# One encoder layer in fp32 on one core: the third group's gMLP split around the prompt output projections, an input of the FFN modulated early, low parts on VectorE

## The chip, the core and the metric

The kernel runs on one core of one Trainium2 chip. The metric is the device time of one execution in microseconds; the median of the runs is given. "TensorE", "VectorE", "ScalarE", "GpSimd" and "SP" are the engines that the profile calls PE, DVE, ACT, POOL and SP.

## What is computed

One layer of a bidirectional encoder, for a prompt of 1024 tokens and a sample of 512 with separate conditions `c` and the same weights. Model width 1024, 12 attention heads of 64 in three dilation groups, four gMLP groups of 64 channels, FFN width 2816. Cut to what matters:

```
h    = rms_norm(x, g_pre_mix) * (1 + sc1) + sh1
proj = h @ w_in                              # q, k, v of the heads; gu, gv of the gMLP
attn = dilated window attention, heads weighted by a softmax over the groups' denominators
gm   = gelu(gu) * (W_s @ layer_norm(gelu(gv)) + b_s)      # in chunks of 128 positions
mix  = concat(attn, gm) @ w_out
x    = x + gt1 * rms_norm(mix, g_post_mix)   # "x1" below
h    = rms_norm(x, g_pre_ffn) * (1 + sc2) + sh2
f    = (silu(h @ w_gate) * (h @ w_up)) @ w_down
y    = x + gt2 * rms_norm(f, g_post_ffn)
```

## The kernel before

**Groups and products.** The 1536 tokens are three groups of 512: 0 and 1 are the prompt, 2 is the sample. Activations lie as eight chunks of 128 channels by 512 tokens. Each fp32 product is made of three matmuls of operands in two parts: `split` (L139) casts the source to the high part on ScalarE (L140) and subtracts it from the source for the low part, on VectorE unless GpSimd is named (L141). Weights are loaded into `wraw`, split into `whl` and used in three matmuls a piece (L158). A matmul's weights, moving operand and result are named in the trace as `pmm<-h,whl`.

**Around the change.** After the attention of group 2 come, on TensorE: the output projection of group 0 (`out_proj(0)`), that of group 1, the whole gMLP of group 2, `out_proj(2)`, and then the first half of the FFN (`ffn_up`). The FFN's first product goes over both prompt groups by a Winograd scheme of seven products of half size: `wino_in` makes its inputs.

- `gmlp` (L728): the v projection (96 matmuls of 128x256), gelu, a normalisation and a split on VectorE, ScalarE and GpSimd (L752 to L762); then the u projection (48 matmuls of 128x512), the mixing over positions (32 matmuls `pst<-qk`), sums (L784), the gate (L787, L791) and two stores into `mix` in DRAM (L792).
- `mix_in` (L867): for each of eight chunks it loads `mix`, for six of them also a reciprocal `rden` and multiplies (L872), then splits into the operands of an output projection, the low part on GpSimd.
- `out_proj` and `post` (L795): eight tiles of the product, evacuated scaled (L808) and squared (L809), the squares summed (L192). A generator goes on in the background: it takes the root, multiplies the eight tiles by it (L821), loads the input, adds it (L822), stores `x1` (L823), squares and sums (L839). At its end stands the root for the FFN's normalisation, `rs2`.
- `wino_in` (L897): for both prompt groups it spreads `rs2`, loads the chunks of `x1`, multiplies them by the root on VectorE (L910), scales and shifts them on ScalarE (L911), forms four sums and differences (`sub`, L894) and splits five of the seven operands (`keep`), three of them with the low part on GpSimd. The other two are stored in DRAM and loaded and split later (`wino_late`).

**What sets the order.** The program is written for a scheduler that puts instructions on each engine in the order of their emission and priority. Background work is a list of generators, `self.back`; `tick(n)` advances the first of them n steps and goes to the next when it is exhausted, and tick(-1) drains all. Tiles come from rings with a fixed number of buffers: three of `xc` (all chunk loads), two of `tb`, two pairs of `st`, four each of `whl` and `wraw`. A load into a ring waits until the tile three (or two, or four) before is done with. SP issues all loads and stores in one order. Later `ada_rest` steps (the conditions' projection, `self.ada`) are filled in between.

## Time and profile before

| | us |
|---|---|
| median of three runs (1874.41, 1874.43, 1877.22) | 1874.43 |
| the profiled execution | 1874.75 |
| its span | 1873.0 |
| TensorE busy | 1808.1 |
| VectorE busy | 1046.9 |
| ScalarE busy | 692.8 |
| GpSimd busy | 145.5 |

The profiled execution is 1.75 us longer than its span. Its mean granted TensorE clock is 0.978. Times of the rows below count from the start of the span. The places: the sample attention ends near 592 us, `out_proj(0)` near 622, `out_proj(1)` at 670, the v and u projections of the third group run from 670 to 694, the mixing from 707 to 719, `out_proj(2)` from 719 to 777, and the FFN after that.

### The profile page before, as it was taken

The page shows a single profiled execution, that of the slowest core. Times are in us where ns is not written, and L with a number is a line of the kernel's source. Part 1 is how long each engine was busy: PE and PEld are TensorE (multiplying, and loading weights), DVE is VectorE, ACT ScalarE, POOL GpSimd, SP SyncE. Part 2 cuts the span into 40 slices and gives each one's busy share as a digit, 9 for nine tenths or more (in the row PEclk, how much of TensorE's full clock was granted, in tenths as well). Part 3 has the DMA queues.
Part 4 walks back from the last instruction along what each step waited for, and adds up shares of the span by engine and source line. Part 5 has one row for each costly group of instructions (what it writes and reads, how often), then busy time and mean ns, then how long its engine had stood idle before and what let it go on. Part 6 is the DMA issues. An engine that isn't in the chain of part 4 may idle for free.

```text
span 1873.0 us, 23145 instructions
## 1 busy us (share of the span) xinstructions
PE 1808.1 (97%) x8602; PEld 1431.1 (76%) x8602; DVE 1046.9 (56%) x1655; ACT 692.8 (37%) x1192; POOL 145.5 (8%) x98
## 2 busy tenths in 40 slices
PE   7999999999999987899999999999999999999997
PEld 7777876776777876677778888878887888888886
DVE  4333964573675566995566766663375374444223
ACT  3611642152335454742232322343345333333232
POOL 0400200010131003400000000000002000000001
PEclk9999999999999997899999999999999999999998
DMA  8112223233363445563321222264365342222432
GB/s 342 34 57 79 91 84 107 102 115 124 102 212 130 136 167 191 181 206 128 111 94 70 79 90 74 73 203 143 103 207 182 96 169 94 92 96 92 139 93 76
DMA packets 125985, 232.47 MB, mean 124 GB/s; under 512 B 14000, under 2 KB 19376, under 8 KB 125872
## 3 DMA queue, kind: packets, MB, share of 16 engines
q1 hardware_dynamic: 125728, 230.93, 36.9%
q8 instruction: 67, 1.10, 0.2%
q14 instruction: 46, 0.38, 0.1%
q10 hardware_dynamic: 144, 0.07, 0.0%
HBM read 196.86 MB, written 34.08 MB: 123 GB/s over the span
## 4 chain that ended last, share of the span: by engine, by line
PE 82%; DVE 7%; DMA 4%; issue 4%; ACT 1%; POOL 1%; DVEq 0%; SPq 0%; POOLq 0%; ACTq 0%
PE pmm L158 66%; PE ppv L158 9%; PE pst L158 7%; DMA xc<-hid 2%; DVE whl L141 1%; DVE sc L587 1%; POOL h L141 1%; DMA xc<-rden 1%; DMA xc<-in_x 1%; DVE sd L587 0%; DVE sc L821 0%; DMA xc<-x 0%; DVE h L141 0%; DVE st L910 0%; DVE acc L192 0%
## 5 line engine op out<-in xcount | busy, mean ns | idle before, releaser
L158 PE MATMUL pmm<-h,whl 128*128 128x512 f32 (+1 forms) x3813 | 946.1, 401 | 13.9 <-ACT h L140 4.6
L158 PEld LDWEIGHTS pmm<-h,whl 128*128 128x128 f32 x3813 | 712.7, 190 | 205.6 <-issue 21.2
L141 DVE TENSOR_TENSOR whl<-wraw,whl 128x512 fp32r<-128x512 f32 (+1 forms) x424 | 293.4, 696 | 315.1 <-ACT whl L140 314.8
L140 ACT CAST whl<-wraw 128x512 fp32r<-128x512 f32 (+1 forms) x424 | 255.9, 607 | 504.9 <-PE pmm L158 373.7
L158 PE MATMUL pmm<-qk,whl 128*128 128x512 f32 x798 | 202.1, 396 | 1.7 <-DVE whl L141 1.6
L158 PEld LDWEIGHTS pmm<-qk,whl 128*128 128x128 f32 x798 | 150.1, 189 | 38.2 <-DVE whl L141 3.0
L158 PE MATMUL ppv<-h,whl 128*128 128x512 f32 x396 | 100.0, 395 | 0.0
L158 PE MATMUL pmm<-v,whl 128*128 128x512 f32 x342 | 90.3, 396 | 0.7 <-DVE st L986 0.7
L158 PEld LDWEIGHTS ppv<-h,whl 128*128 128x128 f32 x396 | 74.5, 188 | 17.5
L158 PE MATMUL pst<-qk 64*128 64x128 f32 (+3 forms) x384 | 65.8, 336 | 17.3 <-DVE qk L141 17.3
L158 PE MATMUL pmm<-h,sc 128*128 128x512 f32 x315 | 80.5, 394 | 0.0
L158 PEld LDWEIGHTS pmm<-v,whl 128*128 128x128 f32 x342 | 64.3, 189 | 18.6 <-ACT whl L140 2.5
L158 PEld LDWEIGHTS pst<-qk 64*128 64x128 f32 (+1 forms) x384 | 48.8, 201 | 38.0 <-issue 32.9
L158 PEld LDWEIGHTS pmm<-h,sc 128*128 128x128 f32 x315 | 59.2, 188 | 13.8
L158 PE MATMUL pmm<-vm,whl 128*128 128x512 f32 x225 | 64.5, 402 | 4.2 <-ACT whl L140 3.9
L192 DVE TENSOR_TENSOR acc<-acc,ta 128x512 f32<-128x512 f32 x55 | 37.8, 687 | 52.3 <-ACT ta L809 42.6
L140 ACT CAST whl<-sd 128x512 fp32r<-128x512 f32 x53 | 32.7, 619 | 83.2 <-PE ppv L158 53.7
L218 POOL TENSOR_TENSOR rq<-rq,half 128x4 f32<-128x4 f32 (+1 forms) x11 | 11.8, 1072 | 585.7 <-DVE rq L217 585.7
L158 PEld LDWEIGHTS pmm<-vm,whl 128*128 128x128 f32 x225 | 42.2, 191 | 18.9 <-ACT whl L140 5.9
L197 POOL PARTITION_ALL_REDUCE acc<-acc x2 | 7.1, 3544 | 578.5 <-DMA xc<-hid 519.3
L462 DVE SCALAR_TENSOR_TENSOR sc<-cst,pst 128x512 f32<-128x512 f32 (+2 forms) x56 | 26.9, 512 | 38.5 <-PE pst L158 38.4
L141 DVE TENSOR_TENSOR whl<-sd,whl 128x512 fp32r<-128x512 f32 x53 | 36.5, 689 | 20.6 <-ACT whl L140 20.6
(241 smaller groups left out, 2012.2 us busy)
## 6 DMA issues: line engine op xcount, KB each, us to landing
wraw<-in_wgu SPq DMA_DIRECT2D x132, 256.0 KB, 2.6
wraw<-in_wdn SPq DMA_DIRECT2D x120, 256.0 KB, 2.6
wraw<-in_win SPq DMA_DIRECT2D x84, 256.0 KB, 2.8
xc<-in_wada SPq DMA_DIRECT2D x48, 256.0 KB, 3.4
wraw<-in_wout SPq DMA_DIRECT2D x48, 256.0 KB, 2.8
sd<-in_wgu SPq DMA_DIRECT2D x44, 256.0 KB, 3.5
xc<-hid SPq DMA_DIRECT2D x44, 256.0 KB, 3.0
xc<-in_x SPq DMA_DIRECT2D x40, 256.0 KB, 3.4
```

The lines of the kernel that those rows point to most:

```text
L140: self.nc.scalar.copy(hi, src)
L141: (eng or self.nc.vector).tensor_tensor(out=lo, in0=src, in1=hi.bitcast(F32), op=ALU.subtract)
L158: self.nc.tensor.matmul(out, lhsT, rhs, start=start, stop=stop, skip_group_check=True)
L192: nc.vector.tensor_tensor(out=acc, in0=acc, in1=t, op=ALU.add)
L197: self.nc.gpsimd.partition_all_reduce(ss, ss, channels=128, reduce_op=RED.add)
L218: nc.gpsimd.tensor_tensor(out=y, in0=y, in1=self.half8[:, :n], op=ALU.pow)
L462: self.nc.vector.scalar_tensor_tensor(out=out, in0=table, scalar=slope, in1=ps, op0=ALU.mult, op1=ALU.add)
L587: nc.vector.tensor_tensor(out=o, in0=o, in1=m, op=ALU.subtract)
```

## The change

1. `gmlp` becomes `gmlp_norm` (v projection, gelu, normalisation, split) and `gmlp_mix` (u projection, mixing, store). For group 2 the first is called right after the sample attention, ahead of `out_proj(0)`, the second after `out_proj(1)`. Groups 0 and 1 call both at once, as before.
2. A new generator, `wino_early`, loads the eight chunks of group 0's `x1`, multiplies them by its root on VectorE, scales and shifts them on ScalarE, into `tb`, and stores them in DRAM (`early`). `wino_in` loads group 0's half from there and modulates group 1's alone (`modulated`).
3. The rest of the `ada` steps and two ticks stand ahead of `out_proj(1)`, and `wino_early` and `mix_in(2)` are put into the background list ahead of it. Before, `mix_in(2)` was put there behind it.
4. The low parts of `mix_in(1)` and `mix_in(2)`, and of three of the five operands in `wino_in`, are made on VectorE: 8 + 8 + 12 instructions. Those of `mix_in(0)` stay on GpSimd.
5. `mix_in(1)` takes its tiles from other rings: three of `qk`, three of `v`, two of `vm`, instead of six and two.

```diff
--- before.py
+++ after.py
@@ -92,6 +92,7 @@
         self.rden = self.dr.tile([NG, 2, 128, TG], F32, name="rden")
         self.x1 = self.dr.tile([NG, 128, KC, TG], F32, name="x1")
         self.hid = self.dr.tile([2, NJ, 128, TG], F32, name="hid")
+        self.early = self.dr.tile([KC, 128, TG], F32, name="early")
         self.late = self.dr.tile([2, 4, 128, TG], F32, name="late")
         self.h = {}
         self.rs2 = {}
@@ -726,6 +727,9 @@
         return t
 
     def gmlp(self, gi, steps):
+        self.gmlp_mix(gi, self.gmlp_norm(gi, steps), steps)
+
+    def gmlp_norm(self, gi, steps):
         nc = self.nc
         self.gmlp_constants()
         wv = [self.weights(self.a["wgv"][i], share=SHARE[2]) for i in range(2)]
@@ -763,6 +767,10 @@
             vh = self.t("qk", [128, 8, 2, 64], F32R)
             self.split(vh[:, :, 0], vh[:, :, 1], w3)
             vhs.append(vh)
+        return vhs
+
+    def gmlp_mix(self, gi, vhs, steps):
+        nc = self.nc
         us = []
         for j in range(2):
             w = self.weights(self.a["win"][18 + j], share=SHARE[2])
@@ -864,14 +872,14 @@
                 eng.tensor_tensor(out=y, in0=y, in1=xs[j][:, :, o], op=ALU.add)
                 nc.sync.dma_start(out=dst[:, 2 * j:2 * j + 2, o], in_=y)
 
-    def mix_in(self, gi, hs, kcs=range(KC), tags=("h",) * KC):
+    def mix_in(self, gi, hs, kcs=range(KC), tags=("h",) * KC, eng=None):
         for kc in kcs:
             x = self.load_chunk(self.mix[gi, kc])
             if kc < 6:
                 r = self.load_chunk(self.rden[gi, kc % 2])
                 self.nc.vector.tensor_tensor(out=x, in0=x, in1=r, op=ALU.mult)
             h = self.t(tags[kc], [128, 2, 512], F32R)
-            self.split(h[:, 0], h[:, 1], x, self.nc.gpsimd)
+            self.split(h[:, 0], h[:, 1], x, eng)
             hs.append(h)
             yield
 
@@ -893,42 +901,53 @@
     def sub(self, out, a, b, eng=None):
         (eng or self.nc.vector).tensor_tensor(out=out, in0=a, in1=b, op=ALU.subtract)
 
+    def wino_early(self):
+
+        rs = self.spread(self.rs2[0], True)
+        for kc in range(KC):
+            x = self.load_chunk(self.x1[0, :, kc])
+            t = self.t2("tb")
+            self.modulated(t, x, rs, kc)
+            self.nc.sync.dma_start(out=self.early[kc], in_=t)
+            yield
+
+    def modulated(self, t, x, rs, kc):
+        self.nc.vector.tensor_tensor(out=t, in0=x, in1=rs, op=ALU.mult)
+        self.nc.scalar.activation(t, t, AF.Identity, bias=self.mod[:, 3, kc, 0:1], scale=self.G[2][:, kc, 0:1])
+
     def wino_in(self, ops):
 
         nc = self.nc
-        rs = [self.spread(self.rs2[gi], True) for gi in range(2)]
+        rs = self.spread(self.rs2[1], True)
         for o in ("B11", "T2", "B21", "T3", "T1", "T4", "B22"):
             ops[o] = []
         for k in range(4):
             B = {}
             for kk in range(2):
                 pair = self.t("st", [128, 2, 512])
-                for gi in range(2):
-                    kc = k + 4 * kk
-                    x = self.load_chunk(self.x1[gi, :, kc])
-                    t = pair[:, gi]
-                    nc.vector.tensor_tensor(out=t, in0=x, in1=rs[gi], op=ALU.mult)
-                    nc.scalar.activation(t, t, AF.Identity, bias=self.mod[:, 3, kc, 0:1], scale=self.G[2][:, kc, 0:1])
-                    B[kk, gi] = t
+                kc = k + 4 * kk
+                nc.sync.dma_start(out=pair[:, 0], in_=self.early[kc])
+                self.modulated(pair[:, 1], self.load_chunk(self.x1[1, :, kc]), rs, kc)
+                B[kk, 0], B[kk, 1] = pair[:, 0], pair[:, 1]
                 yield
             B11, B12, B21, B22 = B[0, 0], B[0, 1], B[1, 0], B[1, 1]
             T = self.t("sd", [128, 3, 512])
             T1, T2 = T[:, 0], T[:, 1]
 
-            def keep(o, src, eng):
+            def keep(o, src):
                 h = self.t(self.OPS[5 * k + ("B11", "T2", "B21", "T3", "T1").index(o)], [128, 2, 512], F32R)
-                self.split(h[:, 0], h[:, 1], src, eng)
+                self.split(h[:, 0], h[:, 1], src)
                 ops[o].append(h)
-            keep("B11", B11, nc.gpsimd)
+            keep("B11", B11)
             self.sub(T1, B12, B11)
             self.sub(T2, B22, T1)
-            keep("T2", T2, nc.vector)
+            keep("T2", T2)
             yield
-            keep("B21", B21, nc.gpsimd)
+            keep("B21", B21)
             self.sub(B12, B22, B12)
-            keep("T3", B12, nc.vector)
+            keep("T3", B12)
             yield
-            keep("T1", T1, nc.gpsimd)
+            keep("T1", T1)
             self.sub(B21, B21, T2)
             nc.sync.dma_start(out=self.late[0, k], in_=B21)
             nc.sync.dma_start(out=self.late[1, k], in_=B22)
@@ -1122,16 +1141,18 @@
         hs = [[], [], []]
         for sp in range(2):
             if sp:
-                self.back.append(self.mix_in(0, hs[0]))
+                self.back.append(self.mix_in(0, hs[0], eng=self.nc.gpsimd))
             self.attention_slot(self.S, sp, STEPS[1])
         self.tick(-1)
-        self.back.append(self.mix_in(1, hs[1], tags=["qk"] * 6 + ["v"] * 2))
+        vhs = self.gmlp_norm(2, GS)
+        self.back.append(self.mix_in(1, hs[1], tags=["qk"] * 3 + ["v"] * 3 + ["vm"] * 2))
         self.out_proj(0, hs[0], 4)
-        self.out_proj(1, hs[1], 4)
         for _ in self.ada:
             pass
-        self.back.append(self.mix_in(2, hs[2], range(6)))
-        self.gmlp(2, GS)
+        self.tick(2)
+        self.back += [self.wino_early(), self.mix_in(2, hs[2], range(6))]
+        self.out_proj(1, hs[1], 4)
+        self.gmlp_mix(2, vhs, GS)
         self.tick(-1)
         for _ in self.mix_in(2, hs[2], range(6, 8)):
             pass
```

The new file's lines are one higher up to L726, then 4, then 8 and more: L821, L822 and L839 become L829, L830 and L847, L872 becomes L880, L894 becomes L902, L910 becomes L915.

How the order of the instructions moves, at three places. First TensorE at the end of the sample attention; `ppv<-sc,v` are its PV products, `pst<-cst,vm` transpositions, `pmm<-h,whl` products of `out_proj(0)`, `pmm<-whl,h` products of the v projection. Before:

```order
L158 MATMUL pmm<-h,whl 128x512 x11
L158 MATMUL ppv<-sc,v 64x192
L158 MATMUL ppv<-sc,ones_82 64x192
L158 MATMUL pmm<-h,whl 128x512 x6
L551 MATMUL pst<-cst,vm 128x128 x4
L158 MATMUL pmm<-h,whl 128x512 x4
L158 MATMUL ppv<-sc,v 64x192
```

Changed:

```order
L159 MATMUL pmm<-whl,h 128x256 x10
L159 MATMUL ppv<-sc,v 64x192
L159 MATMUL ppv<-sc,ones_83 64x192
L159 MATMUL pmm<-whl,h 128x256 x9
L552 MATMUL pst<-cst,vm 128x128 x4
L159 MATMUL pmm<-whl,h 128x256 x11
L159 MATMUL ppv<-sc,v 64x192
```

The v projection of the third group stands between the PV products where products of the first output projection stood.

Second, VectorE behind the u projection of the third group. `xc<-xc` are the multiplications of mix chunks by `rden`, `acc` the gate of the gMLP, `tb<-xc,rs` the modulations of `wino_early`, `h<-xc,h` low parts of mix chunks, and `sc<-sc,rs` the multiplications of the second prompt group. Before:

```order
L787 SCALAR_TENSOR_TENSOR st<-st,row 128x512 x2
L791 SCALAR_TENSOR_TENSOR acc<-st,acc 128x512
L872 TENSOR_TENSOR xc<-xc 128x512
L217 TENSOR_SCALAR rq<-pst 128x4
L723 TENSOR_TENSOR acc<-acc,pmm 128x512
L872 TENSOR_TENSOR xc<-xc 128x512
L725 SCALAR_TENSOR_TENSOR acc<-acc,pmm 128x512
L791 SCALAR_TENSOR_TENSOR acc<-st,acc 128x512
L872 TENSOR_TENSOR xc<-xc 128x512
L141 TENSOR_TENSOR whl<-wraw,whl 128x512 x3
L910 TENSOR_TENSOR st<-xc,rs 128x512 x2
```

Changed:

```order
L915 TENSOR_TENSOR tb<-xc,rs 128x512
L724 TENSOR_TENSOR acc<-acc,pmm 128x512
L915 TENSOR_TENSOR tb<-xc,rs 128x512
L726 SCALAR_TENSOR_TENSOR acc<-acc,pmm 128x512
L880 TENSOR_TENSOR xc<-xc 128x512
L799 SCALAR_TENSOR_TENSOR acc<-st,acc 128x512
L142 TENSOR_TENSOR h<-xc,h 128x512
L880 TENSOR_TENSOR xc<-xc 128x512
L142 TENSOR_TENSOR h<-xc,h 128x512
L142 TENSOR_TENSOR v<-st,v 128x512
L880 TENSOR_TENSOR xc<-xc 128x512
L829 TENSOR_TENSOR sc<-sc,rs 128x512 x8
```

The last of the eight early modulations stand ahead of the first mix chunk, and the eight multiplications of `post(1)` behind the third; before, those and the residual adds stood ahead of the chunks.

Third, SP, which issues the loads into `xc`: `xc<-in_x` are the inputs of the residual adds of `post(1)`, `x_68<-sc` its stores of `x1`, `xc<-x_68` loads of `x1` for `wino_in`. Before:

```order
L239 DMA xc<-in_x 128x512
L823 DMA x_68<-sc 128x512
L239 DMA xc<-mix 128x512
L823 DMA x_68<-sc 128x512
L239 DMA xc<-rden 128x512
L239 DMA xc<-mix 128x512
L239 DMA xc<-rden 128x512
L239 DMA xc<-mix 128x512
L239 DMA xc<-rden 128x512
L239 DMA xc<-mix 128x512
L239 DMA xc<-rden 128x512
L239 DMA xc<-mix 128x512
```

Changed:

```order
L831 DMA x_68<-sc 128x512 x2
L240 DMA xc<-in_x 128x512
L831 DMA x_68<-sc 128x512
L240 DMA xc<-in_x 128x512 x2
L151 DMA wraw<-in_wout 128x512
L831 DMA x_68<-sc 128x512 x2
L240 DMA xc<-mix 128x512
L831 DMA x_68<-sc 128x512
L240 DMA xc<-mix 128x512
L240 DMA xc<-x_68 128x512 x3
```

Before, the loads of the residual adds are followed by those of the mix chunks; now the last two of the eight mix chunks are loaded behind the residual adds, and the loads of `wino_in` behind them.

## Rows read from the trace of the kernel before

**Rows 1.** The page's first part: busy time of each engine, its share of the span, and its number of instructions.

```profile
PE 1808.1 (97%) x8602; PEld 1431.1 (76%) x8602; DVE 1046.9 (56%) x1655; ACT 692.8 (37%) x1192; POOL 145.5 (8%) x98
```

**Rows 2.** The windows of 20 us around the change: window, its length, busy time of PE, PEld, DVE, ACT and POOL with the number of instructions, the granted clock of TensorE (1.00 is 2.4 GHz, 0.50 is 1.2 GHz), the busy share of the DMA engines, GB/s.

```profile
700.00:720.00 20.00, 8.17 (x35) 7.84 (x36) 15.04 (x30) 8.47 (x15) 5.71 (x4) 0.50 0.68 213
...
740.00:760.00 20.00, 15.90 (x62) 12.17 (x61) 16.99 (x24) 15.59 (x27) 9.47 (x4) 0.91 0.58 197
...
780.00:800.00 20.00, 14.62 (x55) 11.27 (x55) 19.50 (x27) 14.68 (x28) 7.41 (x5) 0.74 0.51 170
800.00:820.00 20.00, 16.21 (x58) 12.60 (x59) 19.30 (x33) 8.02 (x14) 0.00 (x0) 0.83 0.54 185
820.00:840.00 20.00, 19.65 (x86) 15.59 (x85) 20.00 (x35) 8.64 (x15) 0.00 (x0) 1.00 0.69 237
```

**Rows 3.** The timeline of TensorE over the same stretch: start, length, engine, line, operation, what it writes from what, shape, count; in brackets the wait ahead of it and what ended it.

```profile
707.17 3.65 PE L158 MATMUL pst<-qk 128*128 128x128 f32 x16 [12.67 <-DVE qk L141]
715.48 3.65 PE L158 MATMUL pst<-qk 128*128 128x128 f32 x16 [4.66 <-DVE qk L141]
...
749.58 0.73 PE L158 MATMUL pmm<-h,whl 128*128 128x512 f32 x2 [3.31 <-ACT whl L140]
751.10 26.46 PE L158 MATMUL pmm<-h,whl 128*128 128x512 f32 x106 [0.79 <-DVE whl L141]
...
784.55 1.84 PE L158 MATMUL pst<-ones,acc 128*128 128x2 f32 x8 [4.93 <-DVE acc L192]
...
803.05 1.22 PE L158 MATMUL pmm<-vm,whl 128*128 128x512 f32 x2 [3.29 <-ACT whl L140]
...
829.86 0.50 PE L158 MATMUL pmm<-vm,whl 128*128 128x512 f32 x1 [0.35 <-DVE whl L141]
```

**Rows 4.** The timeline of VectorE, columns as before: the multiplications (L821) and residual adds (L822) of the second prompt group, the mix chunks' products (L872), the first modulation of the Winograd inputs (L910), eight multiplications of the third group, and the low part that ends TensorE's wait at 829.86. Then a row of GpSimd's timeline: the low part of the last mix chunk.

```profile
693.33 1.88 DVE L822 TENSOR_TENSOR sc<-sc,xc 128x512 f32<-128x512 f32 x3
...
709.71 0.69 DVE L822 TENSOR_TENSOR sc<-sc,xc 128x512 f32<-128x512 f32 x1 [0.80 <-DMA xc<-in_x]
...
714.04 0.69 DVE L872 TENSOR_TENSOR xc<-xc 128x512 f32<-128x512 f32 x1 [0.20 <-DMA xc<-rden]
...
732.58 0.69 DVE L872 TENSOR_TENSOR xc<-xc 128x512 f32<-128x512 f32 x1 [1.96 <-DMA xc<-rden]
...
740.56 1.94 DVE L910 TENSOR_TENSOR st<-xc,rs 128x512 f32<-128x512 f32 x2 [2.66 <-DMA xc<-x]
...
799.47 4.89 DVE L821 TENSOR_TENSOR sc<-sc,rs 128x512 f32<-128x512 f32 x8
...
829.12 0.68 DVE L141 TENSOR_TENSOR whl<-wraw,whl 128x512 fp32r<-128x512 f32 x1
...
740.06 1.29 POOL L141 TENSOR_TENSOR h<-xc,h 128x512 fp32r<-128x512 f32 x1 [3.19 <-ACT h L140]
```

**Rows 5.** Groups of like instructions between 670 and 845 us: line, engine, operation, output from input, shapes, count, then busy time and mean ns of one, and the idle time before them. At the end the row of GpSimd's timeline and of VectorE's that meet.

```profile
L911 ACT ACTIVATE st<-st,mod,G 128x512 f32<-128x512 f32 x16 | 12.6, 813 | 8.9 <-DVE st L910 8.9
L910 DVE TENSOR_TENSOR st<-xc,rs 128x512 f32<-128x512 f32 x16 | 12.5, 807 | 3.8 <-DMA xc<-x 3.1 <-DMA late<-st 0.7
...
L894 DVE TENSOR_TENSOR st<-st,sd 128x512 f32<-128x512 f32 x4 | 4.9, 1226 | 0.0
L894 DVE TENSOR_TENSOR st<-st 128x512 f32<-128x512 f32 x4 | 4.9, 1224 | 0.0
...
L894 DVE TENSOR_TENSOR sd<-st 128x512 f32<-128x512 f32 x4 | 3.8, 950 | 1.0 <-ACT st L911 1.0
...
L894 DVE TENSOR_TENSOR sd<-sd 128x512 f32<-128x512 f32 x4 | 2.7, 680 | 0.0
...
L894 DVE TENSOR_TENSOR ta<-wraw 128x512 f32<-128x512 f32 x2 | 2.4, 1214 | 0.0
...
761.21 1.74 POOL L141 TENSOR_TENSOR qk<-st,qk 128x512 fp32r<-128x512 f32 x1
...
761.71 1.78 DVE L894 TENSOR_TENSOR st<-st 128x512 f32<-128x512 f32 x1
```

**Rows 6.** TensorE's timeline at the end of the second prompt group's output projection: the first part of the third group's v projection, and its u projection.

```profile
669.95 4.73 PE L158 MATMUL pmm<-whl,h 128*128 128x256 f32 x38
...
683.09 11.41 PE L158 MATMUL pmm<-h,whl 128*128 128x512 f32 x48
```

**Rows 7.** The tail of the sample attention: TensorE's timeline (PV products `ppv` among products of the first output projection `pmm`), then two low parts of VectorE's.

```profile
567.96 2.80 PE L158 MATMUL pmm<-h,whl 128*128 128x512 f32 x11
...
572.16 1.67 PE L158 MATMUL pmm<-h,whl 128*128 128x512 f32 x6
...
572.25 0.68 DVE L141 TENSOR_TENSOR whl<-wraw,whl 128x512 fp32r<-128x512 f32 x1
...
576.09 0.68 DVE L141 TENSOR_TENSOR whl<-wraw,whl 128x512 fp32r<-128x512 f32 x1
```

**Rows 8.** DMA issues between 560 and 830 us: output from input, queue, kind, count, KB each, median us from issue to landing.

```profile
xc<-mix SPq DMA_DIRECT2D x11, 256.0 KB, 2.5
late<-st SPq DMA_DIRECT2D x8, 256.0 KB, 2.1
```

## The prediction

> **What bounds the kernel now.** I read the page's first part, then its stretches, then the single waits in the stretch that the change touches. TensorE is busy for 97% of the span [rows 1], so a change can give back only what TensorE loses, and nearly all of the touched loss lies between 694 and 830 us. There the windows [rows 2] show what the whole-span share of 56% for VectorE hides: from 780 on VectorE is busy 19.3 to 20 us of every 20, while TensorE has 14.62 and 16.21 at a clock of 0.74 and 0.83. The waits of TensorE [rows 3] give the places: 12.67 and 4.66 us before the gMLP mixing (both on the low part of the normalised v), 4.93 us for a sum of squares, 3.31 and 3.29 us for weights. The first two stand where the clock is 0.50 [rows 2], 1.2 of 2.4 GHz. After the row at 829.86 TensorE has no wait up to the FFN's steady part: that row waits for the low part of the third FFN tile's first weights, which VectorE gives at 829.12 [rows 3, 4]. **So the shift of that one VectorE instruction is the shift of the end**, unless TensorE has more work ahead of it than VectorE.
>
> What VectorE does before 829.12 begins with the first modulation of the Winograd inputs at 740.56, which waits for a load queued behind the loads of the last mix chunk [rows 4]. In between are 119 VectorE instructions (counted in the order before) in 88.6 us. Eight of a kind take 4.89 us [rows 4], 0.61 each, so 119 x 0.61 = 72.6 us; the other 16 us are contention and waits. Contention: a subtraction alone takes 680 ns; next to GpSimd's low parts the like ones average 1226, 1224 and 950 ns (four each), 1214 (two), and the modulations 807 (16) [rows 5]. The excess is 2.2 + 2.2 + 1.1 + 1.1 + 2.0 = 8.6 us. GpSimd's instruction at 761.21 for 1.74 us and VectorE's at 761.71 for 1.78 show one such meeting [rows 5]; waits are the other 7 us.
>
> **Low parts on VectorE.** Twelve of these move onto VectorE in the Winograd inputs: 12 x 0.61 = 7.3 us added, 8.6 taken away. Eight modulations of group 0 leave the stretch: 8 x 0.61 = 4.9 us less; the order counts 117 instructions up to the same low part, a few others having moved across. Their sum is 117 x 0.61 = 71.4 us instead of 80 with contention. The sixteen low parts of mix chunks that move cost VectorE 0.68 us instead of GpSimd's 1.29 each [rows 4, 5]; eight of them lie under out_proj(0), where TensorE has products for all, so I price those at nothing; if that cover went they would cost 8 x 0.61 = 4.9 us.
>
> Here two pages of the Trainium skill speak. By "SBUF — State Buffer", section "Who interferes with whom", a VectorE instruction with two SBUF inputs and a GpSimd instruction that reads SBUF exclude each other; the 1226 against 680 ns agree. "Perfetto Trace Analysis", section "Optimizing Scalar/DVE Operations", says the opposite of the change: where VectorE is saturated, offload to ScalarE or even GpSimd, though it adds that the two share a port. By it the 7.3 us would be a plain loss; it is a rival below.
>
> **gMLP in two parts.** (a) The v projection's 96 half-width products (38 in 4.73 us [rows 6], so 12.0 us) move from behind out_proj(1) into the tail of the sample attention, where they take the place of out_proj(0) products between the PV products. Their weights' third and fourth low parts stand on VectorE between the attention's probability products, as before at 572.25 and 576.09 [rows 7]. Before, 11 and 6 full-width products ran there, in 2.80 and 1.67 us. In the new order 19 half-width ones stand ahead, 2.4 us, and the next need those weights. I take 4 us of waiting, from 572.16 to 576.09; the bounds are 0 (the low parts come earlier) and 6. So out_proj(1) ends about 4 us later than the v projection ended before, and the u projection begins at 687 instead of 683.09 [rows 6].
> (b) The waits of 12.67 and 4.66 go: v is normalised long before, and mixing follows the u projection directly. TensorE then reaches out_proj(2) near 705 instead of 718.9. What is late next is out_proj(2)'s input, the mix chunks.
>
> **Early modulation.** This sets those chunks. All chunk loads, early loads and residual loads share three xc buffers, in program order on SP and VectorE. The new order is: eight early, chunks 0 to 5, eight residual adds of post(1), chunks 6 and 7, then the Winograd loads. Before, it was eight residual adds, eight chunks, the Winograd loads. So eight loads were put ahead, in a chain that already set the time of 740.56. Step by step:
> - Group 0's root is spread by products that stand behind 17 of the u projection's 48 (48 in 11.41 us [rows 6]): 687 + 4, and one copy, gives the first early modulation at 692.
> - A pair of tb buffers turns over in one VectorE and one ScalarE pass (0.81 each [rows 5]) and a store (2.1 us [rows 8], to 3.5 when loads are queued with it): 1.9 to 2.5 us each. Eight end at 705 to 710; I take 708.
> - Six chunks: before, 714.04 to 732.58 [rows 4], 3.7 us each. A load's 2.5 us [rows 8] and one pass give 3.1 as the lower bound. Eight multiplications of post(1) (4.9 us) now stand between the third and fourth. The last chunk comes at 727 to 734; I take 730.
> - Eight residual adds: before, 693.33 to 709.71 [rows 4], 2.3 us each; 2.0 to 3.0 bound them. They end at 746 to 756; I take 749.
> - Chunks 6 and 7 load (2.5 us [rows 8]) into the buffers so freed and are split: **753, against 741.35 before** (740.06 + 1.29 [rows 4]); bounds 748 to 759.
> - VectorE's first Winograd modulation stands behind the sums of squares of out_proj(2)'s first tiles and ScalarE's copy of group 1's root. Four tiles need chunks 6 and 7, 24 products at 11.41 / 48 = 0.238 (5.7 us), then six evacuation passes on ScalarE of up to 0.81 [rows 5]; as they overlap in part I take 10 us, bounds 7 to 12. First modulation at 763, against 740.56.
>
> **Sum.** 763 + 71.4 + 3 us of waits = 837.4, against 829.1: the end comes 8 us later. For the waits the bounds are 1 (group 0's half is already there) and 7 (as before). TensorE does not decide: out_proj(2) needs 108 products after chunk 7 (26 us), to 779, and the 171 products up to the row that answers to 829.86 take 41 us more at 0.238, to 820. The profiled execution took 1874.75 us, 0.3 above the median of 1874.43. So 1874.43 + 8 = **1882.4 us**. With all lower bounds the sum is 748 + 7 + 71.4 + 1 = 827, 2 us faster; with all upper, 759 + 12 + 71.4 + 7 = 849, 20 slower. Ends all on one side are unlikely, and half the way from 8 to each gives 1877 to 1888.
>
> **Rivals.**
> - *No change (within 0.2%, 3.7 us, about what a measurement of this kernel can tell from nothing).* The chain is only some 8 us late: chunks at 3.1 us, residual loads already in their buffers. First modulation at 754 to 758, and 71.4 + 3 gives 828 to 832: 1873 to 1878. For it: before, those loads waited on buffers, not on bandwidth (DMA share 0.58 to 0.68 [rows 2]).
> - *Faster.* The early loads slip into gaps of xc while TensorE does the u projection and cost the chain nothing; with mixing 14 us earlier, chunk 7 comes at about 741 and the first modulation at 745 to 748. Then 745 + 71.4 + 1 = 817 to 820: 9 to 12 us faster, 1863 at best. For it: 22 us of TensorE's waits (12.67, 4.66, 4.93) would all be gone [rows 3]. Against it: the residual adds cannot pass the chunks on VectorE, and chunk 7 comes behind all of them. It decides where chunk 7 comes before 745.
> - *Slower still, by VectorE.* The low parts add what they take: the slow groups [rows 5] owe their length to something other than GpSimd, and only the 0.61 each is added. The stretch is then about 80 instead of 71.4: 763 + 80 + 3 = 846, 1891. That is what the page on offloading would make of it. Against it: like instructions with GpSimd idle have 680 ns.
> - *That the change does not do what it says:* the order shows that mixing follows the u projection and that the stores and loads of the early part are there, so I give it nothing.
>
> **How the numbers follow.** Forecast with its spread 0.50, slower still 0.08, no change 0.20, faster 0.22. Faster has as much because the chain's sum rests on eight steps, each with several us of bound. The range is 1865 to 1891: it leaves out the better half of the faster case and the tail beyond the slowest. The main case alone has 1877 to 1888. Chances: faster 0.22, the same 0.20, slower 0.58.
>
> **What would show it.** Right: no wait of TensorE before mixing; waits of 3 us and more inside out_proj(2), on the splits of mix chunks and most of all on chunk 6; the first modulation of group 1 near 763; subtractions at 680 ns; VectorE full from there to 837. Also a gap of about 4 us near 572 to 576. Wrong: the last mix chunk split before 745, or TensorE busy without waits from 780 on, which would make it faster; or subtractions still above 900 ns with GpSimd idle, which would make it slower than said.

## The result, and the profile after

The changed kernel takes 1886.43 us (median of six runs, 1883.72 to 1887.13) where the kernel before takes 1874.06 (six runs beside them): a ratio of 1.0066, 95% interval 1.0055 to 1.0076, so 12.4 us slower (10.3 to 14.3). The forecast was 1882.4 in 1865 to 1891. The profiled execution is the fastest of the six, 1883.72 us with a span of 1881.8: 9.0 us above the profiled execution of before. The rows below are of that execution and can explain these 9; what the other 3 are is not shown.

The page's first part and the same windows as in [rows 1, 2]:

```profile
PE 1810.3 (96%) x8602; PEld 1431.2 (76%) x8602; DVE 1053.7 (56%) x1683; ACT 693.4 (37%) x1192; POOL 106.1 (6%) x70
...
700.00:720.00 20.00, 10.03 (x33) 7.72 (x32) 14.09 (x26) 10.01 (x18) 1.39 (x1) 0.59 0.75 234
...
740.00:760.00 20.00, 12.71 (x42) 9.57 (x42) 8.01 (x13) 6.75 (x14) 1.01 (x1) 0.66 0.60 200
...
780.00:800.00 20.00, 13.81 (x46) 9.18 (x45) 19.65 (x35) 14.45 (x26) 8.55 (x1) 0.74 0.56 177
800.00:820.00 20.00, 15.30 (x63) 12.12 (x62) 19.59 (x33) 11.31 (x23) 0.00 (x0) 0.91 0.59 200
820.00:840.00 20.00, 17.05 (x73) 13.50 (x72) 18.45 (x31) 8.76 (x16) 0.00 (x0) 0.98 0.75 257
```

TensorE does the same work. An estimate of what it loses in a window is its idle time plus busy time x (1 - granted clock). Summed over the seventeen windows of 20 us from 560 to 900, that is 59.5 us, 49.5 before, so the loss lies in this stretch. Of the 10 us, 6.1 are lost in 740 to 760 and 4.3 in 820 to 860; what 580 to 600 loses (3.7) is won back in 680 to 720 (6.0). In 740 to 760 VectorE is busy 8.01 us, 16.99 before, while TensorE waits too and has a mean granted clock of 0.66. VectorE's full stretch starts behind that gap.

TensorE's timeline, columns as in [rows 3]: the first row is in the tail of the sample attention, then the u projection (681.85), the mixing, the products for the root of `post(1)`, `out_proj(2)` from 711, and the low parts' two waits in the FFN.

```profile
589.56 10.65 PE L159 MATMUL pmm<-h,whl 128*128 128x512 f32 x38 [2.11 <-DVE whl L142]
...
681.85 4.12 PE L159 MATMUL pmm<-h,whl 128*128 128x512 f32 x17
...
693.90 1.90 PE L159 MATMUL pst<-qk 128*128 128x128 f32 x16
698.13 2.47 PE L159 MATMUL pst<-qk 128*128 128x128 f32 x16 [2.32 <-DVE st L792]
702.35 1.84 PE L159 MATMUL pst<-ones,acc 128*128 128x2 f32 x8 [1.75 <-ACT tb L916]
...
710.61 0.80 PE L159 MATMUL pst<-tb,ones 128*128 128x128 f32 x2 [6.42 <-ACT tb L230]
...
723.59 4.01 PE L159 MATMUL pmm<-h,whl 128*128 128x512 f32 x10 [4.03 <-DVE h L142]
...
749.45 1.84 PE L159 MATMUL pst<-ones,acc 128*128 128x2 f32 x8 [4.42 <-DVE acc L847]
751.68 8.00 PE L159 MATMUL pmm<-h,whl 128*128 128x512 f32 x22 [0.39 <-ACT h L141]
...
814.85 0.50 PE L159 MATMUL pmm<-vm,whl 128*128 128x512 f32 x1 [4.70 <-DVE whl L142]
...
839.10 0.59 PE L159 MATMUL pmm<-vm,whl 128*128 128x512 f32 x1 [2.95 <-DVE whl L142]
```

The last row answers to 829.86 of [rows 3]: 9.24 us later. Of the two waits before the mixing the first is gone (693.90) and the second is down from 4.66 to 2.32 us. In their place are 6.42, 4.03 and 4.42 us on a root, a mix chunk (its low part on VectorE stands behind the eight multiplications of `post(1)`) and the residual's sum of squares. The products for the root of `post(1)` stand at 702.35, behind the mixing; in the kernel before they stood among the v projection's:

```profile
674.52 0.73 PE L158 MATMUL pst<-ones,acc 128*128 128x2 f32 x6
```

VectorE's timeline, answering to [rows 4]: first and last early modulation (L915, `tb`), first mix chunk (L880), the second prompt group's multiplications (L829), last of six chunks, last residual add (L830), low part of the last chunk (`h<-xc,h`), first modulation of the Winograd inputs (L915, `st`), and the low part that ends the wait at 839.10. The last row is ScalarE's: the spreading of the root of `post(1)`.

```profile
687.51 1.29 DVE L915 TENSOR_TENSOR tb<-xc,rs 128x512 f32<-128x512 f32 x2 [1.33 <-ACT rs L235]
...
706.93 0.68 DVE L915 TENSOR_TENSOR tb<-xc,rs 128x512 f32<-128x512 f32 x1
...
709.30 0.69 DVE L880 TENSOR_TENSOR xc<-xc 128x512 f32<-128x512 f32 x1 [0.80 <-DMA xc<-rden]
...
718.03 4.90 DVE L829 TENSOR_TENSOR sc<-sc,rs 128x512 f32<-128x512 f32 x8
...
730.38 0.69 DVE L880 TENSOR_TENSOR xc<-xc 128x512 f32<-128x512 f32 x1 [0.68 <-DMA xc<-rden]
...
747.17 0.69 DVE L830 TENSOR_TENSOR sc<-sc,xc 128x512 f32<-128x512 f32 x1
...
753.43 0.69 DVE L142 TENSOR_TENSOR h<-xc,h 128x512 fp32r<-128x512 f32 x1 [1.01 <-ACT h L141]
...
764.38 1.28 DVE L915 TENSOR_TENSOR st<-xc,rs 128x512 f32<-128x512 f32 x2
...
838.36 0.69 DVE L142 TENSOR_TENSOR whl<-wraw,whl 128x512 fp32r<-128x512 f32 x1
...
710.15 0.40 ACT L230 ACTIVATE tb<-cst,rq 128x128 f32<-128x128 f32 x1 [1.68 <-DMA early<-tb]
```

Read from below: the low part stands 74.0 us behind the first modulation (88.6 before), but that modulation starts 23.8 us later. ScalarE's row shows a step that the prediction did not have: `spread` takes its tile from the ring `tb`, which `wino_early` uses as well, so the root of `post(1)` waits for an early store (the seventh, issued at 707.28 and landed at 710.05). ScalarE stands idle 1.68 us for it, and this ends TensorE's wait of 6.42 us.

Groups of VectorE from 670 to 860, columns as in [rows 5], and two rows of DMA issues as in [rows 8]. The last row is of the kernel before, from the view of [rows 8]: its stores of `x1`.

```profile
L902 DVE TENSOR_TENSOR sd<-st 128x512 f32<-128x512 f32 x4 | 2.7, 684 | 0.6 <-DMA st<-early 0.6
L902 DVE TENSOR_TENSOR st<-st 128x512 f32<-128x512 f32 x4 | 2.7, 684 | 0.0
...
early<-tb SPq DMA_DIRECT2D x8, 256.0 KB, 3.7
...
xc<-mix SPq DMA_DIRECT2D x13, 256.0 KB, 3.2
...
x<-sc SPq DMA_DIRECT2D x22, 256.0 KB, 3.5
```

The subtractions that took 950 and 1224 ns now take 684, as forecast. Early stores land after 3.7 us, not the 2.1 (at most 3.5) assumed. The price of 2.1 was that of the `late` stores, the quicker kind; the stores of `x1` took 3.5 before as well.

### The profile page after: what moved, and what is told of

Its sections match the earlier page's. It is cut to its first block, busy times and chain, and to the rows that moved or that the text cites. A ratio compares the mean times of both kernels' runs of the same rounds, so it can differ in the third digit from the quotient of the medians.

```text
span 1881.8 us, 23182 instructions
## 1 busy us (share of the span) xinstructions
PE 1810.3 (96%) x8602; PEld 1431.2 (76%) x8602; DVE 1053.7 (56%) x1683; ACT 693.4 (37%) x1192; POOL 106.1 (6%) x70
## 4 chain that ended last, share of the span: by engine, by line
PE 56%; issue 33%; DVE 5%; DMA 4%; POOL 1%; ACT 0%; SPq 0%; DVEq 0%; POOLq 0%; ACTq 0%
PE pmm L159 48%; PE pst L159 5%; PE ppv L159 3%; DMA xc<-in_x 1%; POOL h L142 1%; DVE sc L588 1%; DMA xc<-rden 1%; DVE whl L142 1%; DMA h<-in_wada 1%; DVE sc L829 0%; DVE sd L588 0%; DMA early<-tb 0%; DVE h L142 0%; DMA st<-early 0%; PE pst L552 0%
## 5 line engine op out<-in xcount | busy, mean ns | idle before, releaser
L159 PE MATMUL pmm<-qk,whl 128*128 128x512 f32 x726 | 188.3, 401 | 2.9 <-ACT qk L141 1.8
L159 PEld LDWEIGHTS pmm<-qk,whl 128*128 128x128 f32 x726 | 138.2, 191 | 37.1 <-ACT qk L141 2.2
L159 PE MATMUL pmm<-v,whl 128*128 128x512 f32 x366 | 95.2, 394 | 0.7 <-ACT tb L1029 0.7
L159 PE MATMUL pmm<-vm,whl 128*128 128x512 f32 x273 | 76.5, 399 | 10.7 <-DVE whl L142 8.8
L159 PEld LDWEIGHTS pmm<-v,whl 128*128 128x128 f32 x366 | 68.3, 188 | 19.1 <-ACT whl L141 2.5
L159 PEld LDWEIGHTS pmm<-vm,whl 128*128 128x128 f32 x273 | 51.1, 189 | 27.8 <-DVE whl L142 10.4
L219 POOL TENSOR_TENSOR rq<-rq,half 128x4 f32<-128x4 f32 (+1 forms) x11 | 18.8, 1708 | 686.7 <-DVE rq L218 686.7
L1005 DVE TENSOR_TENSOR st<-st,ppv 128x512 f32<-128x512 f32 x44 | 30.1, 685 | 30.8 <-PE ppv L159 30.5
```

What stands on the lines that cost most here:

```text
L159: self.nc.tensor.matmul(out, lhsT, rhs, start=start, stop=stop, skip_group_check=True)
L219: nc.gpsimd.tensor_tensor(out=y, in0=y, in1=self.half8[:, :n], op=ALU.pow)
L1005: add = lambda o, a, b: nc.vector.tensor_tensor(out=o, in0=a, in1=b, op=ALU.add)
```

## The experiments

The theories: **A**, the prediction's: the early part's loads and stores, put ahead in the chain of `xc`, are the loss. **B**: the low parts that VectorE now makes are. **C**: the gMLP in two parts is. **D**: VectorE's full stretch sets the end, so any work taken out of it ahead of the third FFN tile's low part brings the end forward. "Shift" below is that of this low part and of the FFN's last store, in profiled executions, against 829.12 and 1249.69 of before. A profiled execution need not be like the median one. Microseconds behind a ratio are 1875 x (ratio - 1).

**A against B.** `wino_early` is left out, both groups are modulated in `wino_in` as before, and all else stays:

```diff
-        self.back += [self.wino_early(), self.mix_in(2, hs[2], range(6))]
+        self.back.append(self.mix_in(2, hs[2], range(6)))
```

> The changed kernel without the early modulation: wino_in modulates both groups again, all else as changed (gMLP in two parts, mix_in(2) in the background list ahead of out_proj(1), low parts on VectorE). Theory A (the eight early loads ahead of the mix chunks in the three xc buffers made it slower): chunks 0 to 5 are now split under out_proj(1), the residual adds of post(1) end near 707, chunk 7 comes near 715 instead of 753 and the first Winograd modulation near 725 instead of 764. VectorE then has 125 x 0.61 = 76 us and 3 to 6 of waits up to the low part that was at 838: 805 to 812, so 17 to 24 us faster than the kernel before: 1850 to 1857. Theory B (the low parts added on VectorE, on an engine that is full there, made it slower): this kernel has eight VectorE instructions more in that stretch than the changed one and all of its low parts, so it is no faster than the kernel before: 1874 to 1888.

Measured: 1880.1 us, ratio 1.0017 (1.0007 to 1.0026), +3.2 us; shift +1.1 and +2.4. Of the 12.4 us 9 come back; it is still slower than before, where theory A had it 17 to 24 us faster. The time lies in B's range (1874 to 1888), and the next run decides on B. A has a part only.

All 28 low parts go back to GpSimd, the rest of the change stays:

```diff
-            self.split(h[:, 0], h[:, 1], x, eng)
+            self.split(h[:, 0], h[:, 1], x, self.nc.gpsimd)
 ...
-            keep("B11", B11)
+            keep("B11", B11, nc.gpsimd)
 ...
```

(so for B21 and T1.)

> The changed kernel with the 28 low parts back on GpSimd. Theory A: chunk 7 comes at 753 to 756 as in the changed kernel, the first modulation at 764 to 767; VectorE has 105 x 0.61 = 64 us, some 8 us of contention and 3 to 6 us of waits: 839 to 845 against 838, so 1884 to 1891, within 0.3% of the changed kernel (1886). Theory B: the twelve low parts on VectorE cost 12 x 0.61 = 7 us, so 1879 or less.

Measured: 1901.8 us, ratio 1.013 (1.0114 to 1.0146), +24.4; shift +21.6 and +24.3. Its groups from 760 to 860:

```profile
L902 DVE TENSOR_TENSOR st<-st,sd 128x512 f32<-128x512 f32 x4 | 4.9, 1224 | 0.0
...
L902 DVE TENSOR_TENSOR st<-st 128x512 f32<-128x512 f32 x4 | 3.8, 959 | 0.0
L902 DVE TENSOR_TENSOR sd<-st 128x512 f32<-128x512 f32 x4 | 3.8, 955 | 0.1
```

The long subtractions are back as soon as GpSimd works beside them. B has fallen: the low parts on VectorE save 12 us here, more than A's figure (1884 to 1891) allowed. Against the changed kernel the first Winograd modulation comes 4.8 us later (769.18) and the stretch from there to the low part is 7.6 us longer (81.5).

Only the low parts, on the kernel before:

```diff
-            keep("B11", B11, nc.gpsimd)
+            keep("B11", B11, nc.vector)
```

(so for B21, T1 and `mix_in` of groups 1 and 2.)

> The kernel before with only the low parts of mix_in(1), mix_in(2) and wino_in moved to VectorE. Theory A: the first Winograd modulation stays near 740; VectorE has 131 x 0.61 = 79 us up to the low part that was at 829.1 and 3 to 6 us of waits, without contention: 823 to 826, so 3 to 6 us faster than before: 1868 to 1871. Theory B: twelve instructions more on a full VectorE, 7 us slower: 1881.

Measured: 1875.19 us, ratio 0.9988 (0.9979 to 0.9996), -2.3; shift -3.3 and -0.1. A small gain by the medians, below the 3 to 6 us that A had.

Only the gMLP in two parts, on the kernel before, with the tiles of `mix_in(1)`:

```diff
+        vhs = self.gmlp_norm(2, GS)
 ...
         self.out_proj(0, hs[0], 4)
         self.out_proj(1, hs[1], 4)
 ...
-        self.gmlp(2, GS)
+        self.gmlp_mix(2, vhs, GS)
```

> The kernel before with only the gMLP of the third group in two parts (v projection and normalisation ahead of out_proj(0), mixing behind out_proj(1)) and the tiles of mix_in(1) from the other rings, which that needs. mix_in(2) stays behind post(1) in the background list, nothing is modulated early, low parts stay on GpSimd. Theory A: TensorE's waits of 12.7 and 4.7 us before the mixing go, but out_proj(2) waits for the mix chunks, which still follow the residual adds in the xc buffers; these start at 687 to 690 instead of 693, so chunk 7 and the first modulation come 3 to 6 us earlier and the end with them: 1868 to 1872. If the mixing's waits had bounded the end, all 17 us would come back: 1857.

Measured: 1892.55 us, ratio 1.0077 (1.0065 to 1.009), +14.4; shift +15.5 and +17.4. Alone, the part that takes 17 us of waits away costs more than the whole change. A row of TensorE and one of VectorE:

```profile
726.55 1.84 PE L158 MATMUL pst<-ones,acc 128*128 128x2 f32 x8 [20.59 <-DVE acc L846]
...
706.79 4.91 DVE L828 TENSOR_TENSOR sc<-sc,rs 128x512 f32<-128x512 f32 x8 [0.51 <-ACT rs L234]
```

TensorE has run out of other products and waits 20.59 us for the sum of squares behind the residual adds.

**C.** The changed kernel with the gMLP in one piece behind `out_proj(1)` again:

```diff
-        vhs = self.gmlp_norm(2, GS)
 ...
-        self.gmlp_mix(2, vhs, GS)
+        self.gmlp(2, GS)
```

> The changed kernel with the third group's gMLP whole again behind out_proj(1); early modulation, order of the background list and low parts as changed. Theory C: the step that costs is that the v projection's 12 us of TensorE work were moved ahead of out_proj(1), so that the root of post(1), its residual adds and everything behind them come later and nothing covers them; the early loads are cheap where TensorE has the v projection meanwhile. Then the early modulations run from about 671, chunks 0 to 5 end near 705, the residual adds near 722, chunk 7 near 735, the first Winograd modulation near 741, and 74 us behind it (as measured in the changed kernel) the low part at 815 against 829: 1858 to 1866. Theory A (eight more loads through the three xc buffers cost some 16 us wherever they stand): first modulation near 757, 1874 to 1880.

Measured: 1878.73 us, ratio 1.002 (1.0011 to 1.0028), +3.8; shift +4.5 and +6.7 (in an execution of 1885.09, 6.4 us above the median). The time lies in A's range, not in C's.

The same edit on the kernel without `wino_early`:

> The same without the early modulation: gMLP whole behind out_proj(1), mix_in(2) in the background list ahead of out_proj(1), low parts on VectorE. Theory C: residual adds end near 708, mixing near 727, chunk 7 near 733, first Winograd modulation near 735; 86 us behind it (as with the low parts alone) the low part at 821: 1864 to 1870, so 10 to 16 us faster than the same with the gMLP split (1880). Theory A: the split is harmless, the loads' number decides, and both of these have the same loads: 1877 to 1882.

Measured: 1874.51 us, ratio 0.9989 (0.9978 to 1.0001), -2.1; shift -1.9 and -0.5. That is between the two theories: C has the right sign, 5.3 us faster than with the gMLP split where it had 10 to 16, and A's "harmless" has fallen. Neither theory is enough alone. With the low parts on VectorE in all four, the two parts of the change stand so:

| | gMLP whole | gMLP in two parts |
|---|---|---|
| no early part | -2.1 | +3.2 |
| early part | +3.8 | +12.4 |

Two parts cost 5.3 and 8.6 us, the early part 5.9 and 9.2; each entry of the table has an interval of about 2 us to either side, so whether they make each other worse is not settled. The kernel with neither (-2.1) still has the order of the background list and the rings of `mix_in(1)` as changed, and is like the one with the low parts alone (-2.3): those two items cost nothing that can be seen. The cost of the split is seen without the early part, first whole (three rows: the mixing, the multiplications of `post(1)`, the low part of the last mix chunk), then in two parts (the multiplications, and TensorE's wait for a mix chunk):

```profile
720.02 3.65 PE L159 MATMUL pst<-qk 128*128 128x128 f32 x16 [5.52 <-DVE qk L142]
...
690.71 4.29 DVE L829 TENSOR_TENSOR sc<-sc,rs 128x512 f32<-128x512 f32 x7
...
738.04 0.69 DVE L142 TENSOR_TENSOR h<-xc,h 128x512 fp32r<-128x512 f32 x1 [2.77 <-ACT h L141]
```

```profile
712.58 3.10 DVE L829 TENSOR_TENSOR sc<-sc,rs 128x512 f32<-128x512 f32 x5
...
735.11 2.08 PE L159 MATMUL pmm<-h,whl 128*128 128x512 f32 x4 [13.09 <-ACT h L141]
```

Whole, the gMLP comes behind the root of `post(1)`, and the multiplications and residual adds run beside its products. In two parts its v projection stands ahead of `out_proj(1)`, which ends some 11 us later (679.19 against 668.29), and the products for the root come behind the mixing (706.44 against 673.45); the multiplications move from 690.71 to 712.58, and TensorE waits 13.09 us with nothing left to do.

Two cures of that wait, by order. The mix chunks ahead of the early part in the background list:

```diff
-        self.back += [self.wino_early(), self.mix_in(2, hs[2], range(6))]
+        self.back += [self.mix_in(2, hs[2], range(6)), self.wino_early()]
```

> The changed kernel with the two background generators swapped: mix_in(2) ahead of wino_early. Theory A, that the chain of loads through xc sets the end: the chunks no longer wait for group 0's root, so the chain begins at about 676 (as without the early part) instead of 687; chunks 0 to 5 end near 697, the early modulations near 715, the residual adds near 737, chunk 7 near 743, first Winograd modulation near 752 instead of 764: 1873 to 1877. If the start of post(1) sets it instead (theory C, root at about 711 at the earliest, residual adds 18 us behind it and chunks 6 and 7 behind these), the early part is nearly hidden and it is within 4 us of the kernel without it: 1876 to 1884.

Measured: 1885.81 us, ratio 1.0057 (1.0045 to 1.0069), +10.7; shift +9.4 and +10.9. That is above both theories' figures, and no difference from the change itself is shown. The chunks are early (the last of six at 697.88), so the early loads no longer hold them up. What is late is the root of `post(1)`: its tile from `tb` is made at 726.50, behind the early modulations and, for 1.91 us, behind an early store. The multiplications wait for it until 731.69, and the residual adds end at 750.25 (747.86 in the changed kernel).

Without the early part, chunks 6 and 7 ahead of the residual adds:

```diff
-        self.gmlp_mix(2, vhs, GS)
-        self.tick(-1)
+        self.gmlp_mix(2, vhs, 0)
+        self.flush()
         for _ in self.mix_in(2, hs[2], range(6, 8)):
             pass
+        self.tick(-1)
```

(`flush` emits what is still pending, as tick(-1) does first.)

> The kernel of the first series without the early modulation (gMLP in two parts, 1880), with chunks 6 and 7 split ahead of post(1)'s residual adds: the mixing's ticks are put behind them. Theory C says that TensorE's wait of 13.1 us at chunk 6 there is the residual adds' and nothing else: chunk 7 at about 718 instead of 737, out_proj(2) done near 752 instead of 769. The first Winograd modulation stays near 742, since group 1's root waits for the residual adds, but some 16 instructions of VectorE for out_proj(2) (10 us) leave the stretch behind it: low part at 820 to 824 instead of 830, 1870 to 1874. If VectorE's stretch is full whatever stands ahead of it, no gain: 1880.

Measured: 1879.72 us, ratio 1.0022 (1.0011 to 1.0033), +4.1; shift 0.0 and +0.7. The 13.09 us are gone from `out_proj(2)` and stand behind it, ahead of the FFN's first product:

```profile
769.98 1.65 PE L159 MATMUL pmm<-vm,whl 128*128 128x512 f32 x3 [16.52 <-ACT ta L817]
```

`out_proj(2)` sooner is no end sooner. The residual adds of `post(1)` now end at 744.48, 732.71 without this order, and the first Winograd modulation, expected to stay near 742, comes at 750.21 instead of 741.78. The expectation of 1870 to 1874 failed there; its rival, no gain, has the number.

**D.** The background steps of the third group's `post(2)` (multiplications, residual adds, squares) run in the first FFN tiles, on the full VectorE. Here they start at the fourth tile, on the kernel with the gMLP whole and no early part:

```diff
-            self.tick(3)
+            self.tick(3 if j >= 3 else 0)
```

> The kernel with the gMLP whole, without the early modulation and with low parts on VectorE (1874.5), where the background work of post(2) (eight multiplications, eight residual adds, seven sums of the third group, not needed before its FFN) starts behind the fourth FFN tile instead of the first. Theory D: in every kernel of this study TensorE waits last for the first weights' low part of the third FFN tile, because VectorE is full from the first Winograd modulation to there; what is taken out of that stretch comes back at the end. Fourteen to twenty instructions of 0.6 us leave it: low part at 816 to 819 instead of 827, 1863 to 1868. Rival: TensorE is full enough behind 780 that it gains only its listed waits there, 2.2 us: 1872.

Measured: 1868.27 us, ratio 0.9959 (0.9945 to 0.9973), -7.7; shift -17.1 and -11.3. Against the kernel that it is made from (-2.1) the median is 5.6 us better; the low part comes 15.3 us sooner (812.0, where 816 to 819 was expected) and the last store 10.8. The time is at the end of D's range. That TensorE waits last for this low part does not hold in every kernel: with the low parts alone its last wait in this stretch is at 805. The waits that went are these two of that kernel:

```profile
803.81 0.80 PE L159 MATMUL pmm<-vm,whl 128*128 128x512 f32 x1 [4.30 <-DVE whl L142]
...
828.00 0.50 PE L159 MATMUL pmm<-vm,whl 128*128 128x512 f32 x1 [2.24 <-DVE whl L142]
```

The same line in the changed kernel:

> The changed kernel with the same delay of post(2). Theory D: low part at 827 to 830 instead of 838, 1874 to 1878 instead of 1886. Rival: only the last wait of 2.95 us comes back: 1883.

Measured: 1881.55 us, ratio 1.003 (1.0022 to 1.0039), +5.6; shift +2.3 and +7.6. That is 6.8 us better than the change, between D's figure and the rival's.

The same line in the kernel before:

> The kernel before with the same delay of post(2). Theory D: low part at 817 to 821 instead of 829, 1863 to 1868. Rival: before has only 0.35 us of waiting at that place and 4 to 8 us in the stretch ahead of it, of which most stays: 1872 to 1874.

Measured: 1874.84 us, ratio 0.9994 (0.9985 to 1.0003), -1.1; shift -8.9 and -1.9. No gain is shown: the interval holds 1, and the rival was right.

D is right for the low part, three times (-15.3, -6.9, -8.9 against each one's base), and wrong in taking that for the end (last store -10.8, -2.7, -1.9). The gain of the medians is nearly what TensorE no longer waits for. Its waits between 780 and 900 us go from 8.5 to 2.8 us with the gMLP whole (gain 5.6), from 14.1 to 7.6 in the changed kernel (gain 6.8) and from 9.9 to 9.5 in the kernel before (gain 1.1). In these three kernels no wait ends on that low part any more: the last ones ahead of it are at 783, 809 and 800 us, so it no longer sets the pace.

Up to here low part and last store had moved together: between them lie 420.6 us before and 421.3 to 423.8 in the nine other kernels without this line, but 425.8 to 427.5 in these three. Part of that distance is a product of the conditions' projection, `pst<-xc,silz` (and `pst<-tb,silz`); each product shows as two records. Two of its groups between 860 and 880 in the kernel before with the line:

```profile
861.95 1.04 PE L158 MATMUL pst<-xc,silz 128*32 128x512 f32 x2
...
872.18 1.04 PE L158 MATMUL pst<-xc,silz 128*32 128x512 f32 x2
```

and the first in the kernel before itself:

```profile
849.96 1.06 PE L158 MATMUL pst<-xc,silz 128*32 128x512 f32 x6
```

Three products side by side (six records) take what one alone takes. The line scatters them among the steps of `post(2)`, and all such products together cover 11.5 us of TensorE's time, 8.4 before. Other orders scatter them too: of the ten kernels without the line, the four with 8.4 us have distances of 420.6 to 421.9, and the one with 11.5 (low parts alone) has 423.8. The other 4 us of the longer distance are partly the root's products of `post(2)`, now behind the low part, and idle time (1.6 us in the kernel before with the line, 0.35 without).

So the projection's steps were put later too, from the ninth tile, on the kernel of -7.7:

```diff
-            if j >= 4:
+            if j >= 8:
                 next(self.ada, None)
```

> The kernel of the last series with the gMLP whole and post(2) late (1868.3), with the last ada steps begun behind the ninth FFN tile instead of the fifth, so that their loads no longer share the three xc buffers with post(2)'s. Theory E: the 15 us that the low part of the third tile's weights came earlier there (812 against 827) came back only to 11 at the last FFN store, because the ada products, six side by side in 1.06 us before, ran one and two at a time in 0.6 to 1.05 us. In the new order they stand in eight groups again: 3 to 6 us faster, 1862 to 1865. Rival: the difference lies elsewhere (the clock, the spread of runs): 1868.

Measured: 1864.68 us, ratio 0.9941 (0.9927 to 0.9956), -11.1; shift -10.3 and -7.0, in an execution of 1870.05, 5.4 us above the median. The products cover 8.4 us again and the distance is 423.9. That it beats the kernel of -7.7 is not shown: the intervals overlap, and of the profiled executions this one is the slower (1870.05 against 1864.87), with low part and last store 6.8 and 4.3 us later. Theory E is open. The kernel beats the one before by 11 us and, each measured against the kernel before, the changed one by more than 20.

## Why the prediction was right, and where it was not

| step of the prediction | forecast | measured |
|---|---|---|
| wait in the attention's tail | 4, from 572 to 576 | none there; 2.11 at 587 |
| u projection begins | 687 | 681.85 |
| first early modulation begins, last ends | 692, 708 | 687.51, 707.61 |
| last of six mix chunks | 730 | 730.38 |
| last residual add ends | 749 | 747.86 |
| chunk 7 is split | 753 | 754.12 |
| first Winograd modulation | 763 | 764.38 |
| from there to the low part | 74.4 | 74.0 |
| low part | 837.4 | 838.36 |
| shift of the low part | +8 | +9.2 |

- **The sum held** because it went by one chain in absolute times, through the buffers of `xc`. In part that was luck: two misses at its head cancelled. The u projection came 5 us sooner, and the eight early modulations took 20.1 us in place of 16, their stores landing after 3.7 us.
- **The sum's last step held here**: the shift of that low part (+9.2) is near the shift of the FFN's last store (+10.3), and of the profiled time (+9.0). Rows and forecast are of one execution; the median moved by 12.4, and what the 3 us between them are is not shown. As a rule ("the shift of that one VectorE instruction is the shift of the end") the step fails: series D moved the low part by -8.9 us in the kernel before and its median by -1.1.
- **The stretch is no constant.** 71.4 us are 117 instructions (the low part among them), the number for a first modulation near 763; an earlier one has more of VectorE's other work behind it. With all low parts on VectorE there are 116 instructions ahead of the low part in the changed kernel (busy 70.2 us, idle 3.4), 123 with the gMLP whole (74.7, 4.8; modulation at 754.00), and 133 without the early part (80.9, 7.3; at 741.78), of which eight are the modulations that `wino_early` takes out. So the 88.5 us of that last kernel are instructions and waits, and the rivals' sums, which put 71.4 behind a modulation at 745 or 754 as well, are likely too short.
- **The low parts** went as priced: subtractions at 684 ns, a stretch of 74.0 us. In the experiment that puts them back on GpSimd (+24.4, 12 us slower than the change), three groups of like subtractions average 955 to 1224 ns. "SBUF — State Buffer" of the Trainium skill, section "Who interferes with whom", says that a VectorE instruction with two SBUF inputs contends with a GpSimd instruction that reads SBUF, and the runs agree. "Perfetto Trace Analysis" of the Trainium skill, section "Optimizing Scalar/DVE Operations", says that offloading a saturated VectorE may make sense, even to GpSimd, but that between these two it might not help; here it did not.
- **The step that failed is the attribution of the loss to the early part alone** ("eight loads were put ahead, in a chain that already set the time"), with (b), which took the gMLP's split as waits that go and only gave (a) 4 us for it. Left alone, the split loses 5 us, and with the low parts on GpSimd and `mix_in(2)` behind `post(1)` it loses 14. The row for it was there: `out_proj(1)` ends at 669.95 [rows 6], and the split moves that to 681.85. I set the new u projection's start against the old one's (687 and 683.09), not the end of `out_proj(1)` against its own. That end is 12 us later, the products for the root of `post(1)` are 28 us later (702.35 against 674.52), and the products that ran beside its residual adds now lie ahead of it.
- **A step was missing**: the ring `tb`, through which the early stores hold up the root of `post(1)`. What it costs the end is not shown; the wait that it ends is the longest new one of TensorE (6.42 us). Chunk 6, which I named as the likeliest wait, has 0.39.
- **The rivals.** Faster fell by its own sign: chunk 7 came at 753.43, not before 745. Of its 22 us of waits most went, and others came in their place further on. No change fell as well, with the first modulation at 764.38 and not at 754 to 758. Slower still by VectorE fell with the 74 us.

Left open: whether the split and the early part make each other worse, what the ring `tb` costs, and what the 3 us between median and profiled execution are.

## What to carry to other kernels

A wait that is taken from one engine can come back where the next input is late (13.09 us came back as 16.52): price a move by the chain that it delays, and set each product that is moved behind something against its own old time, not its neighbour's. Work put ahead of a product takes its cover away from everything that followed that product's result. Where a ring of buffers is lengthened in its use, list every helper that draws from it, small ones too.

## What the runs showed of the hardware

- Products of 128x32 by 512 ran side by side: three (six records) in 1.06 us, one (two records) in 1.04. "TensorEngine Tiling (Array Packing)" of the Trainium skill, section "Overview", says that the array can be split into independent tiles, and these rows agree. What I had not expected is that scattering these products among other instructions undoes it: they then cover 11.5 us of TensorE's time in place of 8.4.
- Stores of 256 KB do not land alike. In the kernel before the median was 2.1 us for the `late` stores and 3.5 for those of `x1`; in the changed kernel it was 3.5 for both, and 3.7 for the early ones. What makes the difference is not shown.
- In the changed kernel TensorE's granted clock is 0.50 (1.2 GHz) from 744 to 757 us, where it is busy 8.19 of 13.00 us, and 1.00 (2.4 GHz) from 757.5 to 788, where it is busy 28.68 of 30.50. Just before the clock fell TensorE had waited 2.39 us (up to 742.51).
